# Forming half of the low weight parts with an accumulating DMA instead of VectorE

## The chip, the cores and the metric

The kernel runs on one core of one Trainium2 chip. The metric is the device time of one execution in microseconds (us). Engines are named as the profile names them: PE (TensorE, the matrix engine; PEld is its weight load), DVE (VectorE), ACT (ScalarE), POOL (GpSimd) and SP (SyncE). SPq, ACTq and POOLq are the sequencers that issue DMAs; all DMAs run on the core's 16 DMA engines.

## What is computed

Two decoder layers on 256 tokens of width 2048, in float32. Layer 0 mixes tokens by differential attention, layer 1 by a gated linear recurrence; each layer then has a squared-ReLU MLP (2048 to 8192 and back) and a gated embedding. Cut to what matters here:

```
for i in range(DEPTH):                       # DEPTH = 2
    xn = rmsnorm(h, g_mix[i])
    mix = diff_attention(xn, w_qkv, ...) if i % 2 == 0 else rglru_block(xn, w_in, ...)
    h = h + mix                              # both end in a product "@ w_o"
    h = h + square(relu(rmsnorm(h, g_mlp[i]) @ w_up[i])) @ w_down[i]
    ple_gate = sigmoid(rmsnorm(h, g_ple[i]) @ w_ple_gate[i])
    h = h + ple_gate * (p[i] @ w_ple_proj[i])
```

With 256 tokens, each weight is used once and read from memory once; nearly all the work is products with weights.

## The kernel before

**Precision.** A float32 operand is split into a high part (rounded to the short mantissa of float32r) and a low part, the rest. A product is then three matmuls, hi·hi, hi·lo and lo·hi. Line numbers are those of the profile of the kernel before.

**Tiling.** A `Group` (L60) is one product of 256 tokens with 512 columns. Its weights come in `Chunk`s of four k-tiles (512 rows of 512 columns, 1 MB), each loaded by one DMA on SP (L351) into a raw tile `w_raw`, of which there are three. A chunk is used as two `Sub`s of two k-tiles; the text calls them its even half (k0 = 0) and its odd half (k0 = 2). Each half is split into `w_hi` and `w_lo` tiles of 128x1024 elements, of which there are four each. `split` (L253) does that: ACT casts `w_raw` to `w_hi` (L255), and DVE subtracts, `w_lo = w_raw - w_hi` (L256).

**Order of the work.** `stream` (L332) walks over the halves of all groups. At half j it asks for loads two chunks ahead (L371), then for the split of half j + 3 (`split_to`, L374), then issues the matmuls of half j. With four buffers, the split of half j + 3 writes the tiles that the matmuls of half j - 1 have read, so it can start when these have ended, and must be done when the matmuls of half j + 3 begin: three halves later. In the products of the layout `flip` (L378, the MLP's up products) a half is 16 matmuls with the weights as the stationary operand; in the others (`mm3`, L248) it is 12 matmuls with the weights as the moving operand. Evictions, transposes, norms and softmax are deferred by some halves (`defer`, L115), so that they fall between the matmuls of later halves. Within the order in which the code is recorded, a scheduler may move instructions on DVE, ACT, PE and POOL; each engine then runs its own list in that order.

POOL does little: constants, the `rstd` powers of the norms (L265, L267, L310), and a few small loads (L150, L199, L413).

Some halves are not split this way: gate weights of layer 1 go through `own` (L887, a chunk without a source array), and the small `w_ple_proj` chunks have an even half only.

Of the kernel before, what the change touches and what calls it, by code (L numbers as in the profile page):

```python
# [11 lines left out]
AF = mybir.ActivationFunctionType  # L12
ALU = mybir.AluOpType
# [4 lines left out]
P = 128  # L18
# [9 lines left out]
EPS = 1e-6  # L28
KT_D = D // P
KC = 4  # L30
SK = 2
# [9 lines left out]


class Chunk:
    """Up to KC k-tiles of one weight column block, moved by one DMA."""

    def __init__(self, src, nk):
        self.nk, self.raw, self.pre = nk, None, None
        self.pieces = [(lambda raw: raw[:, :nk], src)]


class Sub:
    """SK k-tiles of a chunk, split into two float32r parts."""

    own = None

# [2 lines left out]


class Group:  # L60
    """One product over nk k-tiles: [256 tokens, 512 columns], or its transpose where flip is set."""

    def __init__(self, w, k0, nk, n0, lhs, evict, flip=False):
        self.lhs, self.evict, self.nk, self.flip, self.subs, self.pre = lhs, evict, nk, flip, [], {}
# [9 lines left out]
def trunk_kernel(ctx: ExitStack, tc, a, out):  # L74
    nc = tc.nc
# [4 lines left out]
    wk = ctx.enter_context(tc.tile_pool(name="wk", bufs=2))  # L80

    def t4(shape, dtype=F32):
        """4 KiB a partition"""
        return wk.tile(shape, dtype, tag="t4", name="t4", bufs=3)

    def v4(shape, dtype=F32):
# [6 lines left out]
        return wk.tile(shape, dtype, tag="t1", name="t1", bufs=3)  # L93

    def big(shape, dtype=F32):
        """8 KiB a partition"""
        return wk.tile(shape, dtype, tag="big", name="big", bufs=4)

    sm = ctx.enter_context(tc.tile_pool(name="sm", bufs=4))
# [7 lines left out]
    x = a["x"][0]  # L107
    p = a["p"]
    o_v = out[0].rearrange("(t p) d -> p t d", p=P)

# [1 line left out]
    state = {"tick": 0}  # L112
    pending = []

# [9 lines left out]
                pending.remove(e)  # L124
                e[2]()

# [1 line left out]
    h = cp.tile([P, NT, D], F32, name="h")  # L128
    x_v = x.rearrange("(t p) d -> p t d", p=P)

# [62 lines left out]
        nc.vector.tensor_scalar_mul(gss, g_sub, 1.0 - LAM0)  # L193

    def lam_setup():
        """lambda of the differential attention, the same on every partition"""
        lamv = t2([P, 4, DK])
        for i, nm in enumerate(("lam_q1", "lam_k1", "lam_q2", "lam_k2")):
            nc.gpsimd.dma_start(lamv[:, i], a[nm][0].partition_broadcast(P))  # L199

        def finish():
            lamm = t1([P, 2, DK])
            nc.vector.tensor_tensor(lamm, lamv[:, 0::2], lamv[:, 1::2], op=ALU.mult)
            lams = sm.tile([P, 2], F32, name="lams", bufs=1)
            nc.vector.tensor_reduce(lams, lamm, axis=AX.X, op=ALU.add)
            lame = sm.tile([P, 2], F32, name="lame", bufs=1)
            nc.scalar.activation(lame, lams, AF.Exp)
            nc.vector.tensor_tensor(neg_lam, lame[:, 1:2], lame[:, 0:1], op=ALU.subtract)
            nc.vector.tensor_scalar(neg_lam, neg_lam, LAM0, None, op0=ALU.subtract)

        defer(4, finish)

    def mask_setup():
        """-(query - key) where the key is visible, else a huge negative number"""
        nc.gpsimd.iota(
            mtab, pattern=[[-P, NT], [1, SEQ]], base=0, channel_multiplier=-1, allow_small_or_imprecise_dtypes=True
        )
        nc.gpsimd.affine_select(
            mtab, mtab, pattern=[[P, NT], [-1, SEQ]], compare_op=ALU.is_ge, fill=NEG, base=0, channel_multiplier=1
        )  # L220

    # 8 * softplus(-lam): log1p(u) = 2 atanh(u / (2 + u)) with u = exp(-|lam|)
    sp8 = cp.tile([P, 16], F32, name="sp8")
    nsp8 = cp.tile([P, 16], F32, name="nsp8")

# [18 lines left out]
        nc.vector.tensor_scalar_mul(sp8, ser, 8.0)  # L244
        nc.vector.tensor_scalar_mul(nsp8, ser, -8.0)

# [1 line left out]
    def mm3(ps, lh, ll, rh, rl, start, stop):  # L248
        nc.tensor.matmul(ps, lhsT=lh, rhs=rh, start=start, stop=False)  # L249
        nc.tensor.matmul(ps, lhsT=lh, rhs=rl, start=False, stop=False)  # L250
        nc.tensor.matmul(ps, lhsT=ll, rhs=rh, start=False, stop=stop)  # L251

    def split(hi, lo, src):  # L253
        """src = hi + lo exactly, each part of float32r's 12 significant bits."""
        nc.scalar.copy(hi, src)  # L255
        nc.vector.tensor_tensor(lo, src, hi.bitcast(F32), op=ALU.subtract)  # L256

# [2 lines left out]
        nc.vector.scalar_tensor_tensor(lo, in0=src, scalar=scale, in1=hi.bitcast(F32), op0=ALU.mult, op1=ALU.subtract)  # L260

    def rstd(ss, n, width, name):
        """(ss / width + EPS) ** -0.5 of [P, n]"""
        m = sm.tile([P, n], F32, name=name + "_m")
        nc.gpsimd.tensor_scalar(m, ss, 1.0 / width, EPS, op0=ALU.mult, op1=ALU.add)  # L265
        r = sm.tile([P, n], F32, name=name + "_r")
        nc.gpsimd.tensor_tensor(r, m, mhalf[:, :n], op=ALU.pow)  # L267
        return r

    def x32(shape):  # L270
        """32 KiB a partition"""
        return xp.tile(shape, F32R, tag="x32", name="x32")

    class Operand:
        """A split [k, token] operand of nk k-tiles."""

        def __init__(self, hi, lo):
            self.hi, self.lo = hi, lo
# [2 lines left out]
            return self.hi[:, kt, t * P : (t + 1) * P], self.lo[:, kt, t * P : (t + 1) * P]  # L281

    class Wide(Operand):
        """Both parts of a k-tile side by side: one [k, 512] moving operand."""

        def __init__(self):
            self.both = x32([P, KT_D, 2, SEQ])
            self.hi, self.lo = self.both[:, :, 0], self.both[:, :, 1]

    class Norm(Wide):  # L290
        """The rmsnorm of h as a transposed, split operand; the row factor r goes onto the products."""

        def __init__(self, gcol):
            super().__init__()
# [33 lines left out]
            for b in range(2):  # L328
                defer(1 + b, lambda b=b: self.transpose(nb, b))

# [1 line left out]
    def stream(groups):  # L332
        subs = [s for g in groups for s in g.subs]
        chunks = []
# [19 lines left out]
        def split_to(i):  # L354
            while done["split"] < min(i + 1, len(subs)):
                s = subs[done["split"]]
                load_to(cidx[id(s.chunk)])
                if s.own is not None:
                    s.own(s)
                else:  # L360
                    s.hi = wsp.tile([P, SK, NB], F32R, name="w_hi")
                    s.lo = wsp.tile([P, SK, NB], F32R, name="w_lo")
                    split(s.hi, s.lo, s.chunk.raw[:, s.k0 : s.k0 + SK])
                done["split"] += 1

        j = 0
        for g in groups:
            acc = [psum([P, NB]) for _ in range(4 if g.flip else NT)]
            kt = 0
            for i, s in enumerate(g.subs):  # L370
# [7 lines left out]
                if g.flip:  # L378
                    x = g.lhs()
                    for f in range(4):  # L380
                        fs = slice(f * P, (f + 1) * P)
                        for kk in range(SK):
                            k = kt + kk
# [10 lines left out]
                else:  # L394
                    for t in range(NT):
                        for kk in range(SK):
                            k = kt + kk
# [7 lines left out]

    groups = []

# [1 line left out]
    pT = {}  # L409

    def p_setup(l):
# [10 lines left out]

        defer(4, transpose)

# [1 line left out]
    n0 = Norm(G_MIX)  # L426

    attnT = [[big([P, 4, 3, P], F32R) for _ in range(2)] for _ in range(2)]
# [37 lines left out]
        return evict  # L466

    def softmax(ps, heads, t, nk):
        """attn = softmax(c = 0) - lam * softmax(c = 1) of [P, heads, 2, nk] scores"""
        n = len(heads)  # L470
        s = t2([P, n, 2, nk])
        for i, hd in enumerate(heads):
            nc.vector.scalar_tensor_tensor(
                s[:, i],
                in0=mtab[:, t, :nk].unsqueeze(1).broadcast_to([P, 2, nk]),
                scalar=2.0 ** -(hd + 1),
                in1=ps[:, i],
                op0=ALU.mult,
                op1=ALU.add,
            )  # L480
        s2 = s.rearrange("p n c k -> p (n c) k")
        nm = sm.tile([P, 2 * n], F32, name="nm")
        nc.vector.tensor_reduce(nm, s2, axis=AX.X, op=ALU.max)
        nc.vector.tensor_scalar_mul(nm, nm, -1.0)
        z = sm.tile([P, n, 2], F32, name="z")
        zf = z.rearrange("p n c -> p (n c)")
        for i in range(2 * n):
            nc.scalar.activation(s2[:, i], s2[:, i], AF.Exp, bias=nm[:, i : i + 1], accum_out=zf[:, i : i + 1])
        nc.vector.reciprocal(zf, zf)
        nc.vector.tensor_scalar_mul(z[:, :, 1], z[:, :, 1], neg_lam)  # L490
        at = t1([P, n, nk])
        for i in range(n):
            nc.vector.tensor_scalar_mul(s[:, i, 1], s[:, i, 1], z[:, i, 1:2])
            nc.vector.scalar_tensor_tensor(
                at[:, i], in0=s[:, i, 0], scalar=z[:, i, 0:1], in1=s[:, i, 1], op0=ALU.mult, op1=ALU.add
            )
        return at
# [93 lines left out]
                )  # L591

    def residual_evict(nb, norm, scale=None):
        """h += product; the last contribution to this block feeds the next norm."""

        def evict(acc):
            add_to_h(acc, nb, scale)
            if norm is not None:
                norm().feed(nb)

        return evict
# [20 lines left out]
    for nb in range(4):  # L622
        groups.append(Group(a["w_o_attn"][0], 0, KT_D, nb * NB, lambda kt, t: oT().lhs(kt, t), residual_evict(nb, n_mlp0)))

# [1 line left out]
    FC = 1024  # L626
    NFC = DFF // FC
    FKT = FC // P
# [1 line left out]
    def mlp(l, norm_in, norm_out):  # L630
        hid = {}

        def up_evict(c, half):
            """relu(.) ** 2 of a transposed product; the row factor squared goes onto the next product"""

            def evict(acc):
                if half == 0:
# [32 lines left out]
            down(c - 1)  # L670
        down(NFC - 1)

# [1 line left out]
    def ple(l, norm_in, norm_out):  # L674
        pps, sgs = {}, {}

# [45 lines left out]
    n_mix1 = later(lambda: Norm(G_MIX + 16))  # L722
    ple(0, n_ple0, n_mix1)

# [1 line left out]
    w_in = a["w_in_rec"][0]  # L726
    rg = {}
    yT = later(Wide)
# [5 lines left out]
        return rg  # L734

    def gate_weights():
        """They lie in the k-tiles of yT that come last."""
        w = yT().both[:, 8:16]
        return w[:, :, 0], w[:, :, 1]

# [61 lines left out]
        return evict  # L802

    def recur(half):
        """a = exp(-s r), b = sqrt(1 - a^2) i x with 1 - a^2 = tanh(s r) (1 + a^2); then the scan"""

        def decay(q):
            for c in range(4 * q, 4 * q + 4):
# [62 lines left out]
        return evict  # L871

    def gate_chunk(nb):
        """The gate weights of 512 channels: they go through the weight stream's loads and splits."""
        ch = Chunk(None, KC)
        v = lambda raw: raw.rearrange("p k n -> p (k n)").rearrange("p (n g k j) -> p n g k j", n=2, g=2, k=2)
        ch.pieces = [
# [1 line left out]
                lambda raw, n=n, g=g: v(raw)[:, n, g],  # L879
# [28 lines left out]
    mlp(1, n_mlp1, n_ple1)  # L908
    ple(1, n_ple1, None)

    # the first group takes x as it comes
    first = groups[0]
    chunks = [first.subs[i].chunk for i in range(0, len(first.subs), KC // SK)]
    w0 = w_qkv[: KC * P, :NB].rearrange("(c p) n -> p c n", p=P)
# [62 lines left out]
```

## Time and profile before

| | |
|---|---|
| median of 3 timed runs | 2328.12 us (2327.57 to 2328.15) |
| span of the profiled execution (its own time, first to last instruction) | 2326.8 us |
| PE busy | 2308.8 us, 99% |
| DVE busy | 1424.6 us, 61% |
| ACT busy | 1193.6 us, 51% |
| POOL busy | 44.7 us, 2% |
| weight loads on SP (queue q1), share of 16 DMA engines | 57.3% |
| read from HBM | 435 MB |

The table gives shares of the whole span. An engine at 99% sets the time; the others cost only where PE waits for them. The profile shows this with its idle times: PE's groups have almost none before them.

### The profile page before, as it was taken

The numbers are of one execution on the slowest core, as the hardware profiler recorded it, in microseconds if no ns is written. First come the engines' busy times: TensorE is split into PE (matmuls) and PEld (weight loads), VectorE is DVE, ScalarE is ACT, GpSimd is POOL, SyncE is SP. The second block draws the span as 40 slices with busy tenths as digits, with TensorE's granted clock in tenths as the row PEclk, the third lists the DMA queues.
The fourth block names the chain that finished last, engine by engine and source line by source line (L and its number), as shares of the span: only waits on it lengthen the run. The fifth ranks groups of instructions, "written<-read, shape, count | busy, mean of one in ns | idle before, by whom it ended". The sixth has DMA issues, their size and how long they took to land.

```text
span 2326.8 us, 28564 instructions
## 1 busy us (share of the span) xinstructions
PE 2308.8 (99%) x11467; PEld 1946.9 (84%) x11467; DVE 1424.6 (61%) x1704; ACT 1193.6 (51%) x1594; POOL 44.7 (2%) x79
## 2 busy tenths in 40 slices
PE   8999999999999999999999999999999999999999
PEld 6888888888888888888888887888888888888887
DVE  6676655565565665566566767566565555565654
ACT  6555554444444444444558887454444444444453
POOL 2100000000000000000000000000000000000000
PEclk9999999999999999999999999999999999999999
DMA  7454555555565655655566565556565565555554
GB/s 241 163 185 163 165 179 181 185 195 189 191 197 184 198 188 192 196 185 181 189 193 219 187 212 181 181 182 198 184 197 190 191 197 184 198 189 191 177 199 148
DMA packets 225396, 438.95 MB, mean 189 GB/s; under 512 B 7582, under 2 KB 16416, under 8 KB 225264
## 3 DMA queue, kind: packets, MB, share of 16 engines
q1 hardware_dynamic: 224608, 436.24, 57.3%
q8 instruction: 89, 1.46, 0.3%
q0 software_dynamic: 608, 0.89, 0.2%
q14 instruction: 43, 0.35, 0.0%
q10 hardware_dynamic: 48, 0.02, 0.0%
HBM read 435.01 MB, written 2.10 MB: 188 GB/s over the span
## 4 chain that ended last, share of the span: by engine, by line
PE 94%; DVE 2%; ACT 2%; DMA 1%; issue 1%; SPq 0%; POOL 0%; DVEq 0%; ACTq 0%
PE acc L391 31%; PE acc L251 21%; PE acc L249 20%; PE acc L250 20%; PE tp L317 1%; DVE w_lo L256 1%; ACT w_hi L255 1%; DMA w_raw<-in_w_gate_x_dram 0%; DVE t L770 0%; DMA h<-in_x_dram 0%; PE tp L458 0%; DVE big L827 0%; ACT L810 0%; SPq L351 0%; ACT L788 0%
## 5 line engine op out<-in xcount | busy, mean ns | idle before, releaser
L256 DVE TENSOR_TENSOR w_lo<-w_raw,w_hi 128x1024 fp32r<-128x1024 f32 x808 | 987.4, 1224 | 781.4 <-ACT w_hi L255 779.9
L255 ACT CAST w_hi<-w_raw 128x1024 fp32r<-128x1024 f32 x808 | 849.0, 1052 | 979.8 <-PE acc L251 605.7
L391 PE MATMUL acc<-x,w_hi 128*128 128x512 f32 x2048 | 704.8, 394 | 0.0
L391 PE MATMUL acc<-x,w_lo 128*128 128x256 f32 x2048 | 547.8, 278 | 0.0
L249 PE MATMUL acc<-w_hi,x 128*128 128x512 f32 x1152 | 457.1, 397 | 0.0
L250 PE MATMUL acc<-w_lo,x 128*128 128x512 f32 x1152 | 450.2, 391 | 1.9 <-DVE w_lo L256 1.8
L251 PE MATMUL acc<-w_hi,x 128*128 128x512 f32 x1152 | 450.5, 391 | 0.0
L391 PEld LDWEIGHTS acc<-x,w_hi 128*128 128x128 f32 x2048 | 376.0, 188 | 78.6
L249 PE MATMUL acc<-w_hi,big 128*128 128x512 f32 x1024 | 399.7, 390 | 0.0
L251 PE MATMUL acc<-w_hi,big 128*128 128x512 f32 x1024 | 398.6, 389 | 0.0
L250 PE MATMUL acc<-w_lo,big 128*128 128x512 f32 x1024 | 398.4, 389 | 0.0
L391 PEld LDWEIGHTS acc<-x,w_lo 128*128 128x128 f32 x2048 | 384.7, 188 | 11.2
L251 PEld LDWEIGHTS acc<-w_hi,x 128*128 128x128 f32 x1152 | 216.8, 188 | 46.8 <-DVE x L256 0.2
L250 PEld LDWEIGHTS acc<-w_lo,x 128*128 128x128 f32 x1152 | 217.2, 189 | 45.0 <-DVE w_lo L256 3.0
L249 PEld LDWEIGHTS acc<-w_hi,x 128*128 128x128 f32 x1152 | 216.8, 188 | 41.7
L251 PEld LDWEIGHTS acc<-w_hi,big 128*128 128x128 f32 x1024 | 192.2, 188 | 40.3
L250 PEld LDWEIGHTS acc<-w_lo,big 128*128 128x128 f32 x1024 | 192.3, 188 | 39.8
L249 PEld LDWEIGHTS acc<-w_hi,big 128*128 128x128 f32 x1024 | 192.2, 188 | 39.0
L589 DVE SCALAR_TENSOR_TENSOR h<-acc,n_r,h 128x512 f32<-128x512 f32 x128 | 89.9, 744 | 0.0
L644 ACT COPY t<-acc 128x256 f32<-128x256 f32 x128 | 47.5, 371 | 22.8 <-PE acc L391 20.6
L259 ACT ACTIVATE x<-tp,cols_a 128x256 fp32r<-128x256 f32 (+1 forms) x72 | 35.7, 496 | 39.5 <-DVE x L260 39.5
L260 DVE SCALAR_TENSOR_TENSOR x<-tp,cols_a,x 128x256 fp32r<-128x256 f32 (+1 forms) x72 | 36.8, 511 | 18.8 <-ACT x L259 18.8
(173 smaller groups left out, 1064.2 us busy)
## 6 DMA issues: line engine op xcount, KB each, us to landing
w_raw<-in_w_up_dram SPq DMA_DIRECT2D x128, 1024.0 KB, 5.2
w_raw<-in_w_down_dram SPq DMA_DIRECT2D x128, 1024.0 KB, 5.1
w_raw<-in_w_qkv_dram SPq DMA_DIRECT2D x47, 1024.0 KB, 5.2
w_raw<-in_w_ple_gate_dram SPq DMA_DIRECT2D x32, 1024.0 KB, 5.2
w_raw<-in_w_in_rec_dram SPq DMA_DIRECT2D x32, 1024.0 KB, 5.5
w_raw<-in_w_o_attn_dram SPq DMA_DIRECT2D x16, 1024.0 KB, 5.2
w_raw<-in_w_o_rec_dram SPq DMA_DIRECT2D x16, 1024.0 KB, 5.1
w_raw<-in_w_ple_proj_dram SPq DMA_DIRECT2D x8, 512.0 KB, 3.7
```

The costliest lines, as they stand in the source:

```text
L249: nc.tensor.matmul(ps, lhsT=lh, rhs=rh, start=start, stop=False)
L250: nc.tensor.matmul(ps, lhsT=lh, rhs=rl, start=False, stop=False)
L251: nc.tensor.matmul(ps, lhsT=ll, rhs=rh, start=False, stop=stop)
L255: nc.scalar.copy(hi, src)
L256: nc.vector.tensor_tensor(lo, src, hi.bitcast(F32), op=ALU.subtract)
L259: nc.scalar.activation(hi, src, AF.Copy, scale=scale)
L260: nc.vector.scalar_tensor_tensor(lo, in0=src, scalar=scale, in1=hi.bitcast(F32), op0=ALU.mult, op1=ALU.subtract)
L317: nc.tensor.transpose(tp[:, i, t * P : (t + 1) * P], h[:, t, (k0 + i) * P : (k0 + i + 1) * P], ident)
L391: nc.tensor.matmul(o, lhsT=lh, rhs=rh, start=k == 0 and n == 0, stop=k == g.nk - 1 and n == 1)
L589: nc.vector.scalar_tensor_tensor(hb, in0=acc[t], scalar=scale()[:, t : t + 1], in1=hb, op0=ALU.mult, op1=ALU.add)
L644: nc.scalar.copy(other, ps[:, SEQ:])
```

## The change

The weight source is kept in the chunk. For the even half nothing changes. For the odd half of every chunk that has a source array, three operations stand where two stood: ACT writes the negated rounded weights into `w_lo` (L367 of the changed kernel), ACT casts the same raw weights into `w_hi` (L368), and POOL issues a DMA (L369) that reads the same 128x2x512 weights from HBM once more and adds them to `w_lo`, so that `w_lo = -hi + w`. The subtraction on DVE is gone for these halves. The rest of the diff drops docstrings and comments; lines behind L369 are six higher than before.

```
     def __init__(self, src, nk):
-        self.nk, self.raw, self.pre = nk, None, None
+        self.nk, self.raw, self.pre, self.src = nk, None, None, src
...
                     s.hi = wsp.tile([P, SK, NB], F32R, name="w_hi")
                     s.lo = wsp.tile([P, SK, NB], F32R, name="w_lo")
-                    split(s.hi, s.lo, s.chunk.raw[:, s.k0 : s.k0 + SK])
+                    raw = s.chunk.raw[:, s.k0 : s.k0 + SK]
+                    if s.k0 == 0 or s.chunk.src is None:
+                        split(s.hi, s.lo, raw)
+                    else:
+                        nc.scalar.activation(s.lo, raw, AF.Copy, scale=-1.0)
+                        nc.scalar.copy(s.hi, raw)
+                        nc.gpsimd.dma_start(s.lo, s.chunk.src[:, s.k0 : s.k0 + SK], accum_op=ALU.add)
                 done["split"] += 1
```

How the instructions move is shown at three places. The first is ACT in the MLP of layer 0, around the eviction of an up product (`t1<-acc` are its copies, `big` the split of its result); a raw tile's number tells which two halves belong to one chunk. Before:

```order
L255 CAST w_hi_5305<-w_raw_5283 128x1024
L255 CAST w_hi_5327<-w_raw_5283 128x1024
L255 CAST w_hi_5347<-w_raw_5325 128x1024
L644 COPY t1_5370<-acc_5195 128x256
L644 COPY t1_5373<-acc_5196 128x256
L644 COPY t1_5380<-acc_5197 128x256
L644 COPY t1_5383<-acc_5198 128x256
L255 CAST w_hi_5395<-w_raw_5325 128x1024
L255 CAST big_5367<-t2_5369 128x512
L255 CAST w_hi_5415<-w_raw_5393 128x1024
```

And the same place in the changed kernel:

```order
L255 CAST w_hi_5413<-w_raw_5390 128x1024
L367 ACTIVATE w_lo_5436<-w_raw_5390 128x1024
L368 CAST w_hi_5435<-w_raw_5390 128x1024
L255 CAST w_hi_5456<-w_raw_5433 128x1024
L650 COPY t1_5479<-acc_5300 128x256
L650 COPY t1_5482<-acc_5301 128x256
L650 COPY t1_5489<-acc_5302 128x256
L367 ACTIVATE w_lo_5505<-w_raw_5433 128x1024
L650 COPY t1_5492<-acc_5303 128x256
L368 CAST w_hi_5504<-w_raw_5433 128x1024
L255 CAST big_5476<-t2_5478 128x512
L255 CAST big_5476<-t2_5488 128x512
```

ACT has three operations of 128x1024 for a chunk in place of two; the negated copy stands ahead of the cast of the same half.

The second place is ACT at the start of the program, where the first chunks are split (the difference of the two lists; `h` is the residual stream, `n_ss` the sums of squares of the first norm):

```order
 L302 ACTIVATE t_150,n_ss<-h 128x512
-L255 CAST w_hi<-w_raw 128x1024 x3
+L367 ACTIVATE w_lo<-w_raw 128x1024
+L368 CAST w_hi<-w_raw 128x1024
+L255 CAST w_hi<-w_raw 128x1024
+L368 CAST w_hi<-w_raw 128x1024
+L367 ACTIVATE w_lo<-w_raw 128x1024
 L259 ACTIVATE x_101<-tp,cols_g 128x256
```

The first odd half's negated copy stands where its cast stood; in the second chunk the cast comes first.

The third place is POOL in the attention's projections (`q_m`, `q_r` and `o_m` are the powers of the norms; all `w_lo` rows are accumulating DMAs):

```order
+L369 DMA w_lo<-in_w_qkv_dram 128x2x512 x4
 L265 TENSOR_SCALAR q_m<-q_ss 128x8
 L267 TENSOR_TENSOR q_r<-q_m,mhalf 128x8
+L369 DMA w_lo<-in_w_qkv_dram 128x2x512 x4
 L265 TENSOR_SCALAR q_m<-q_ss 128x8
 L267 TENSOR_TENSOR q_r<-q_m,mhalf 128x8
+L369 DMA w_lo<-in_w_qkv_dram 128x2x512 x4
```

POOL's list has 400 rows more, all accumulating DMAs; they stand in the same list as the norms' powers. The list of SP's loads keeps its order.

## Rows read from the trace of the kernel before

**Rows 1.** The page: busy time, share of the span and instructions of each engine.

```profile
PE 2308.8 (99%) x11467; PEld 1946.9 (84%) x11467; DVE 1424.6 (61%) x1704; ACT 1193.6 (51%) x1594; POOL 44.7 (2%) x79
```

**Rows 2.** The page's groups: line, engine, op, out<-in, xcount | busy us, mean ns | idle before.

```profile
L256 DVE TENSOR_TENSOR w_lo<-w_raw,w_hi 128x1024 fp32r<-128x1024 f32 x808 | 987.4, 1224 | 781.4 <-ACT w_hi L255 779.9
L255 ACT CAST w_hi<-w_raw 128x1024 fp32r<-128x1024 f32 x808 | 849.0, 1052 | 979.8 <-PE acc L251 605.7
...
L250 PE MATMUL acc<-w_lo,x 128*128 128x512 f32 x1152 | 450.2, 391 | 1.9 <-DVE w_lo L256 1.8
```

**Rows 3.** The chain that ended last: start us, length us, what (longest pieces).

```profile
537.50 44.40 PE acc L391 x256
625.42 44.40 PE acc L391 x256
...
2088.84 44.40 PE acc L391 x256
```

**Rows 4.** Timeline of ACT and DVE within an MLP: start us, length us, engine, line, operation.

```profile
1004.90 1.05 ACT L255 CAST w_hi<-w_raw 128x1024 fp32r<-128x1024 f32 x1 [1.10 <-PE acc L391]
1005.98 1.23 DVE L256 TENSOR_TENSOR w_lo<-w_raw,w_hi 128x1024 fp32r<-128x1024 f32 x1 [0.94 <-ACT w_hi L255]
1007.67 1.05 ACT L255 CAST w_hi<-w_raw 128x1024 fp32r<-128x1024 f32 x1 [1.72 <-PE acc L391]
```

**Rows 5.** DMA queues and issues in the MLP's window 460 to 1047 us.

```profile
q1 hardware_dynamic: 56337, 111.88, 58.4%
...
w_raw<-in_w_down_dram SPq DMA_DIRECT2D x57, 1024.0 KB, 5.2
w_raw<-in_w_up_dram SPq DMA_DIRECT2D x50, 1024.0 KB, 5.2
```

**Rows 6.** Stretches: window, length, busy PE, PEld, DVE, ACT, POOL, PEclk, DMA share, GB/s.

```profile
5.00:10.00 5.00, 1.42 (x6) 0.72 (x4) 2.68 (x4) 2.36 (x4) 3.06 (x6) 1.00 1.02 343
10.00:15.00 5.00, 3.69 (x11) 3.13 (x12) 0.88 (x2) 2.56 (x7) 0.09 (x1) 1.00 1.05 390
460.00:1047.00 587.00, 587.00 (x2998) 499.87 (x2998) 346.63 (x378) 259.31 (x298) 0.00 (x0) 1.00 0.59 191
1215.00:1460.00 245.00, 240.88 (x1187) 201.15 (x1186) 174.47 (x230) 197.88 (x282) 1.93 (x7) 1.00 0.61 198
```

**Rows 7.** DMA issues of the whole span: KB each, median us from issue to landing.

```profile
w_raw<-in_w_ple_proj_dram SPq DMA_DIRECT2D x8, 512.0 KB, 3.7
...
h<-in_x_dram SPq DMA_DIRECT2D x3, 512.0 KB, 11.2
...
t<-in_p_dram POOLq DMA_DIRECT2D x2, 256.0 KB, 3.4
```

**Rows 8.** POOL's issue of the load of p: duration ns min/median/max.

```profile
L413 POOL DMA_DIRECT2D t<-in_p_dram x2: 778/789/800, 133.9 to 1191.9; - x2
```

**Rows 9.** Timeline of the start: splits and first matmuls.

```profile
14.39 2.94 ACT L255 CAST w_hi<-w_raw 128x1024 fp32r<-128x1024 f32 x3
...
15.46 3.50 DVE L256 TENSOR_TENSOR w_lo<-w_raw,w_hi 128x1024 fp32r<-128x1024 f32 x3 [1.64 <-ACT w_hi L255]
...
17.44 0.71 PE L249 MATMUL acc<-w_hi,x 128*128 128x512 f32 x2
```

**Rows 10.** Groups of ACT and DVE in layer 1's mixer, 1215 to 1460 us.

```profile
L255 ACT CAST w_hi<-w_raw 128x1024 fp32r<-128x1024 f32 x77 | 79.9, 1048 | 25.8 <-PE acc L251 25.4
...
L822 ACT ACTIVATE big<-big 128x1024 f32<-128x1024 f32 x4 | 4.2, 1058 | 0.0
...
L256 DVE TENSOR_TENSOR w_lo<-w_raw,w_hi 128x1024 fp32r<-128x1024 f32 x76 | 92.1, 1221 | 32.7 <-ACT w_hi L255 32.7
```

**Rows 11.** Groups of ACT in the window 460 to 1047 us.

```profile
L255 ACT CAST w_hi<-w_raw 128x1024 fp32r<-128x1024 f32 x214 | 225.5, 1054 | 318.4 <-PE acc L251 164.6 <-PE acc L391 153.8
```

## The prediction

> **What bounds the kernel now.** I read the busy times first: PE is busy 2308.8 us of a span of 2326.8, DVE 61%, ACT 51%, POOL 2% [rows 1]. Only 18 us are left in which PE does nothing, so no relief of another engine can give back more than that. The page's groups say the same from the other side: the matmuls that read w_lo waited 1.8 us in all for DVE's subtraction, while DVE itself idled 781 us waiting for ACT's cast, and ACT idled 980 us, mostly until PE set a buffer free [rows 2]. So the split runs ahead of PE and is held back by it. The chain of waits gives the pace in the MLPs: 256 matmuls of an up product pair (16 halves) take 44.40 us, 2.775 us a half, and the next such piece starts 87.92 us after the last, 32 halves later: 2.75 us a half on average, 5.495 us a chunk [rows 3]. The MLPs have 256 of the 400 chunks that the change touches. The timeline shows the reserve of the split there. The cast starts when PE ends half j - 1, the subtraction ends 2.31 us later (1004.90 to 1007.21) [rows 4], and the result is wanted when half j + 3 starts, 3 x 2.75 = 8.25 us after the cast's start: 5.9 us to spare.
>
> The DMA engines come next, since the change puts its load there. In the window 460 to 1047 us the weight loads fill 58.4% of all 16 engines with 107 chunks, so one chunk takes 0.584 x 587 / 107 = 3.20 us of the 16 engines [rows 5]. At the start, when the engines are full (shares 1.02 and 1.05), they move 343 and 390 GB/s, by which a chunk of 1.049 MB takes 3.06 or 2.69 us [rows 6].
>
> **What goes.** 400 subtractions on DVE of 1.224 us [rows 2], 490 us of busy time, beside a PE that does not wait for them: worth nothing in the MLPs, and at most the 18 us of PE's idle time anywhere.
>
> **What comes on ACT.** 400 negated copies. The operation with a scale is not in the trace on this shape; the cast of the same shape takes 1.054 us [rows 11] and an activation of that shape in layer 1's mixer 1.058 [rows 10], so I take 1.06. In an MLP that is 107 x 1.06 = 113 us on top of 259 in 587 us [rows 6]: 63%, covered by ACT's 318 us of waiting for PE there [rows 11]. In layer 1's mixer (1215 to 1460 us) it is not covered so well: 77 casts mean some 38 odd halves, 40 us on top of 198 in 245 [rows 6, 10], so ACT is at 97% while PE already has 4 us of idle time there. Bounds: minus 4 (DVE loses 38 x 1.22 = 46 us there, and PE's idle time goes) to plus 40 (none of the new copies finds a gap). I take 2, since ACT's wait for PE before the casts alone is 25.8 us there and there are further waits to fill.
>
> **What comes on POOL.** 400 issues. POOL's own issue of a 256-row transfer takes 0.79 us [rows 8]; one per 5.5 us fills 14% of an almost empty engine. Each issue waits for its negated copy, and the norms' powers queue behind it. They wait for at most one such copy and issue, some 2 us, and the factors are wanted at an eviction several halves away: nothing.
>
> **What comes on the DMA engines.** 400 transfers of 512 KB, 210 MB on top of 435. The accumulating form does not stand in the trace, so its cost is bounded. From below: it costs what a plain transfer of 512 KB does, half a chunk, 1.35 to 1.60 us of the 16 engines. Together with the chunk's load 4.04 to 4.80 us, below the pace of 5.495: hidden. The middle value: an addition needs the old w_lo as well as the weights, two operands of 512 KB for one result, so it costs the engines what 1 MB costs, 2.69 to 3.20 us; with the load 5.38 to 6.40 us against 5.495, which is at the edge or over it. From above: nothing in the rows excludes a slower path still; the slowest 512 KB transfer, the load of x into full queues, took 11.2 us to land [rows 7]. I take the middle value, because it follows from what the operation must read, and the rows for it are the 1 MB loads.
>
> The Trainium skill, page "Collectives: The Full Stack", section "The bandwidth ceiling: the fold count and why AG ≠ RS ≠ AR", says of additions in the DMA path that the add itself costs no cycles, but that its two source reads go through one ring, so that it delivers half the rate of a copy. No run here shows an accumulation so far; the plain row of 512 KB above would let the change end near 2333 us, the rule at the sum below.
>
> **The wait that decides.** The chain of an odd half is now: PE ends half j - 1, negated copy 1.06, DMA from issue to landing L, then PE's own half 2.75, and four halves of PE must hold this: 4 x 2.75 = 11.0. So the change is hidden as long as L is at most 11.0 - 1.06 - 2.75 = 7.2 us; beyond it the chunk takes (3.81 + L) / 2. A plain 512 KB transfer lands in 3.7 us [rows 7], a 1 MB one in 5.2 [rows 5]. The accumulation does not run alone: the load into the raw tile that this same half sets free is issued within about a microsecond of it, and shares all 16 engines. A plain cost gives L = 3.7 + 1.35 to 1.60 = 5.1 to 5.3, hidden with 1.9 to spare. The double cost gives L = 5.2 + 2.69 to 3.20 = 7.9 to 8.4, so the chunk takes 5.85 to 6.1 us, 0.36 to 0.61 more than now. Over 256 chunks that is 91 to 156 us; I take the middle, 124. The other 144 chunks have (2326.8 - 256 x 5.495) / 144 = 6.4 us each, or 6.2 without the start and the few small chunks, because PE does transposes, scores and gates between their halves: 5.85 to 6.1 us fits, and I count nothing.
>
> **The start.** The first chunks are split while PE waits for them. The second half's w_lo is ready at about 16.6 us (15.46 and one subtraction) and its matmuls begin about 17.4 [rows 9]. In the changed order the negated copy stands in the cast's place, ends at 15.4, and the DMA lands 5.2 to 8.4 us later among full queues, at 20.6 to 23.8: PE begins 3.2 to 6.4 us later, and since it never waits again, the loss stays. I take 5.
>
> **The sum.** 2326.8 + 124 + 5 + 2 = 2457.8. The profiled execution's span stands 1.3 us below the median of the runs shown; with that the forecast is 2459 us, PE waiting for accumulating DMAs.
>
> **The rivals.**
> Hidden: the accumulation costs about what a copy costs, L stays near 5, and PE keeps its pace in the MLPs. For it: PE's reserve of 5.9 us and 41.6% free DMA time. Against it: the start and the mixer still cost something, 0 to 10 us in all. That gives 2328 to 2340 us; I split it into no change (2328) and a small loss, which reaches 2400 if some transfers land late.
> Slower path: accumulation takes several times a copy. With L = 11.2 a chunk takes 7.5 us: 256 x 2.0 + 144 x 1.3 = 700 us more, 3030. For it: nothing in the trace shows the form, and its result is rounded to another type on the way. Against: L must be over three times that of a plain 512 KB.
> Faster: in layer 1's mixer DVE's share falls, PE's 4.1 us of idle time there go, and with them some 3 of the other 14 at the start and the end. It decides only if the accumulation is cheap enough to stay hidden everywhere (L below 7.2) and the start loses nothing; then 2328.1 - 7 = 2321 us. Against it: ACT, not DVE, is the fuller engine there, and it is ACT that gets the copies.
> That the change does not do what it says I rule out: 400 transfers more stand in POOL's list and 400 subtractions fewer in DVE's.
>
> **How the numbers follow.** Forecast (DMA path at double cost, 2400 to 2600; its ends are the cheapest wait above, and a queue held at 6.40 us a chunk, 256 x 0.9 + 144 x 0.2 = 260 more): 0.47. Hidden, a small loss of 2333 to 2400: 0.22. Hidden, no change: 0.15. Slower path, beyond 2600: 0.13. Faster: 0.03. What can be told from no change is 0.2%, 4.7 us. So faster 0.03, same 0.15, slower 0.47 + 0.22 + 0.13 = 0.82. The range that holds 8 in 10 takes the forecast, the small losses, half of no change and the lower half of the slower path: 2328 to 2720.
>
> **What would show it.** The profile after should show 400 w_lo DMAs on a POOL queue with about 210 MB; DVE's L256 down to 408 and ACT up by about 420 us; DMA share above 90% in the MLPs; PE idle before the matmuls that read w_lo, released by DMA w_lo, in odd halves alone; a chunk of 5.85 to 6.1 us where it was 5.5; and landings of 7.9 to 8.4 us. Landings near 5 us with PE still at 99% would make the forecast wrong by the step on double cost; landings well above 9 us would make it wrong by the same step on the other side. PE waits that name ACT in the mixer beyond a few us would upset that term.

## The result and the profile after

The changed kernel takes 2821.03 us (median of 4 runs, 2813.96 to 2831.86) against 2327.85 us: 1.2122 times as long (95% interval 1.2096 to 1.2148), 493 us more. The forecast was 2459 us and slower; the sign was right, the size was not, and the range (to 2720) did not hold it. The profiled execution has a span of 2812.1 us at a mean granted clock of 0.975.

The page before has this chain by engine (the shares of the work that ended last):

```profile
PE 94%; DVE 2%; ACT 2%; DMA 1%; issue 1%; SPq 0%; POOL 0%; DVEq 0%; ACTq 0%
```

The page after: busy times (they answer to [rows 1]), the two DMA queues (q1 has SP's loads, q0 POOL's transfers), the chain by engine, DVE's subtractions, and two groups of matmuls that read w_lo ([rows 2] has one of them before).

```profile
PE 2441.1 (87%) x11467; PEld 1986.9 (71%) x11467; DVE 967.8 (34%) x1304; ACT 1553.7 (55%) x1992; POOL 519.7 (18%) x479
...
q1 hardware_dynamic: 224608, 436.24, 49.5%
q0 software_dynamic: 109408, 210.63, 42.5%
...
DMA 55%; PE 27%; issue 10%; ACT 7%; DVE 1%; POOL 1%; SPq 0%; POOLq 0%; ACTq 0%; DVEq 0%
...
L256 DVE TENSOR_TENSOR w_lo<-w_raw,w_hi 128x1024 fp32r<-128x1024 f32 x408 | 499.5, 1225 | 1442.0 <-ACT w_hi L255 1441.5
...
L397 PE MATMUL acc<-x,w_lo 128*128 128x256 f32 x2048 | 571.4, 289 | 115.7 <-DMA w_lo<-in_w_up_dram 115.2
...
L250 PE MATMUL acc<-w_lo,big 128*128 128x512 f32 x1024 | 414.2, 405 | 120.4 <-DMA w_lo<-in_w_down_dram 120.0
```

The 400 subtractions are gone as counted (987.4 to 499.5 us in DVE's group). The busy time of DVE as a whole fell by 457 us and that of ACT rose by 360, less than the 490 and 420 that were counted. But the chain that was 94% PE is now 55% DMA, and the matmuls that read w_lo, which had waited 1.8 us for DVE, now wait more than 230 us for the accumulating DMAs in these two groups alone. By q0's share an accumulation takes 0.425 x 2812.1 / 400 = 2.99 us of the 16 engines; by q1's share and its 436 MB a chunk's load of 1.049 MB takes about 3.35.

The loads of w_down in layer 0 give the pace: issues by line, with first and last start. First the kernel before:

```profile
L351 SPq DMA_DIRECT2D w_raw<-in_w_down_dram x64: 367/368/368, 474.4 to 1084.3; - x64
```

Then the changed kernel:

```profile
L351 SPq DMA_DIRECT2D w_raw<-in_w_down_dram x64: 367/368/368, 538.7 to 1294.4; - x64
```

The same stretch of work takes 755.7 us in place of 609.9; at 5.495 us a chunk before [rows 3] that is 6.81 us a chunk.

The four pairs of `w_hi` and `w_lo` buffers are used in turn, each again after four halves; the text calls this the ring. A transfer has landed when its semaphore says that the data are there. One turn of the ring can be read in the timeline of the changed kernel. The rows are the negated copy of an odd half, the issue of its DMA, the first matmul that reads its w_lo, and the next negated copy into the same buffer.

```profile
1005.24 1.06 ACT L367 ACTIVATE w_lo<-w_raw 128x1024 fp32r<-128x1024 f32 x1 [1.77 <-PE acc L250]
...
1006.60 1.19 POOL L369 DMA_DIRECT2D w_lo<-in_w_down_dram  x1 [4.83 <-ACT w_lo L367]
...
1015.95 0.50 PE L250 MATMUL acc<-w_lo,big 128*128 128x512 f32 x1 [1.67 <-DMA w_lo<-in_w_down_dram]
...
1018.57 1.06 ACT L367 ACTIVATE w_lo<-w_raw 128x1024 fp32r<-128x1024 f32 x1 [3.44 <-PE acc L250]
```

Copy 1.06, handing over 0.30, DMA from 1006.60 to about 1015.8, the half on PE, and the buffer is free 13.3 us after the copy began. Four halves of PE take 11.0. The prediction's ring is there, with a longer DMA in it: two chunks in 13.3 us are 6.7 us a chunk.

### The profile page after: what moved, and what is told of

Same layout as the page of the kernel before. It is cut to its first block, busy times and chain, and to the rows that moved or that the text cites. A ratio compares the mean times of both kernels' runs of the same rounds, so it can differ in the third digit from the quotient of the medians.

```text
span 2812.1 us, 29666 instructions
## 1 busy us (share of the span) xinstructions
PE 2441.1 (87%) x11467; PEld 1986.9 (71%) x11467; DVE 967.8 (34%) x1304; ACT 1553.7 (55%) x1992; POOL 519.7 (18%) x479
## 4 chain that ended last, share of the span: by engine, by line
DMA 55%; PE 27%; issue 10%; ACT 7%; DVE 1%; POOL 1%; SPq 0%; POOLq 0%; ACTq 0%; DVEq 0%
DMA w_lo<-in_w_down_dram 20%; DMA w_lo<-in_w_up_dram 19%; PE acc L250 7%; PE acc L397 7%; PE acc L251 6%; PE acc L249 6%; ACT w_lo L367 5%; DMA w_lo<-in_w_qkv_dram 4%; DMA w_lo<-in_w_ple_gate_dram 4%; DMA w_lo<-in_w_in_rec_dram 3%; DMA w_lo<-in_w_o_attn_dram 2%; DMA w_lo<-in_w_o_rec_dram 2%; DMA w_raw<-in_w_gate_x_dram 1%; ACT w_hi L255 0%; DVE w_lo L256 0%
## 5 line engine op out<-in xcount | busy, mean ns | idle before, releaser
L256 DVE TENSOR_TENSOR w_lo<-w_raw,w_hi 128x1024 fp32r<-128x1024 f32 x408 | 499.5, 1225 | 1442.0 <-ACT w_hi L255 1441.5
L367 ACT ACTIVATE w_lo<-w_raw 128x1024 fp32r<-128x1024 f32 x400 | 424.2, 1060 | 783.1 <-PE acc L250 511.6
L397 PE MATMUL acc<-x,w_hi 128*128 128x512 f32 x2048 | 732.6, 403 | 0.0
L397 PE MATMUL acc<-x,w_lo 128*128 128x256 f32 x2048 | 571.4, 289 | 115.7 <-DMA w_lo<-in_w_up_dram 115.2
L250 PE MATMUL acc<-w_lo,x 128*128 128x512 f32 x1152 | 470.4, 408 | 113.5 <-DMA w_lo<-in_w_in_rec_dram 31.2
L250 PE MATMUL acc<-w_lo,big 128*128 128x512 f32 x1024 | 414.2, 405 | 120.4 <-DMA w_lo<-in_w_down_dram 120.0
L249 PE MATMUL acc<-w_hi,x 128*128 128x512 f32 x1152 | 464.7, 405 | 0.0
L251 PE MATMUL acc<-w_hi,x 128*128 128x512 f32 x1152 | 462.1, 401 | 0.0
L368 ACT CAST w_hi<-w_raw 128x1024 fp32r<-128x1024 f32 x400 | 414.4, 1036 | 15.6 <-PE acc L251 15.6
L369 POOL DMA_DIRECT2D w_lo<-in_w_down_dram x128 | 152.7, 1193 | 722.5 <-ACT w_lo L367 608.4
L369 POOL DMA_DIRECT2D w_lo<-in_w_up_dram x128 | 152.6, 1192 | 711.9 <-ACT w_lo L367 562.6
L251 PEld LDWEIGHTS acc<-w_hi,x 128*128 128x128 f32 x1152 | 224.2, 195 | 46.3
L249 PEld LDWEIGHTS acc<-w_hi,x 128*128 128x128 f32 x1152 | 223.2, 194 | 45.1
```

What stands on the lines that cost most here:

```text
L367: nc.scalar.activation(s.lo, raw, AF.Copy, scale=-1.0)
L368: nc.scalar.copy(s.hi, raw)
L369: nc.gpsimd.dma_start(s.lo, s.chunk.src[:, s.k0 : s.k0 + SK], accum_op=ALU.add)
L397: nc.tensor.matmul(o, lhsT=lh, rhs=rh, start=k == 0 and n == 0, stop=k == g.nk - 1 and n == 1)
```

## The experiments

**Adding against copying.** The first two runs vary what the DMA does.

```
-  nc.gpsimd.dma_start(s.lo, s.chunk.src[:, s.k0 : s.k0 + SK], accum_op=ALU.add)
+  nc.gpsimd.dma_start(s.lo, s.chunk.src[:, s.k0 : s.k0 + SK])                    # copy_not_add
+  nc.gpsimd.dma_start(s.lo, raw, accum_op=ALU.add)                               # add_from_raw
```

> The DMA of the odd half copies the weights into w_lo instead of adding them to it (so w_lo is not the low part; what is left out is the addition alone). Issue, waits, bytes read from HBM and bytes written stay. Theory A, the addition is what is dear, because it needs two operands: a transfer takes the engines half of the 2.99 us that it takes now, about 1.5, landing falls from 9.0 to about 6 us, a chunk goes back to 5.5 us in the MLPs, and the time to 2330 to 2360 us. Rival B, the queue of POOL (its issue of 1.19 us, its way of making descriptors) is what is dear: landing stays at 8 to 9 us and the time at 2700 to 2820 us.

Measured: 2418.14 us, 1.0389 times before (1.0359 to 1.0419), 403 us less than with the addition. So the accumulating form is most of the price. Its page has the queues and the landings:

```profile
q1 hardware_dynamic: 224608, 436.24, 49.4%
q0 software_dynamic: 109408, 210.63, 36.0%
...
w_lo<-in_w_up_dram POOLq DMA_DIRECT2D x128, 512.0 KB, 4.5
w_lo<-in_w_down_dram POOLq DMA_DIRECT2D x128, 512.0 KB, 6.5
```

The same bytes take 0.360 x 2417.3 / 400 = 2.18 us of the engines, not the 1.5 that was expected, and the time missed the expected 2330 to 2360. Rival B (2700 to 2820) is refuted; whether the queue has a share in the 90 us that are left, no run separates.

> The accumulating DMA takes its weights from the raw tile in SBUF, not from HBM a second time. Theory A, the price is the two operands that each engine must read, wherever they lie: engine time per transfer stays near 3 us and the time at 2700 to 2830 us. Rival C, the second reading of HBM is the price (645 MB in place of 435): engine time falls towards 2 us, landing to about 7, and the time to 2340 to 2500 us. The raw tile is held until the DMA has landed, so if loads become late as well the time can rise above 2830.

Measured: 2600.72 us, 1.1173 times before (1.1078 to 1.1269), between both expectations. The engine time of a transfer stays (43.3% of 2608.3 us, 2.82 us each), as theory A has it: reading SBUF in place of HBM does not make the addition cheap for the engines. But it lands in 6.1 us in the median, not 9.0, and now ACT waits for late loads as well (119.0 and 100.2 us before w_hi, for the loads of w_down and w_up), since the raw tile must be held until the DMA has read it. Engine time and time to land are two things.

**Why it lands late.** The DMA view of short windows of the changed kernel, after the issue at 1006.60 above. First 1008.0 to 1010.4 us, then 1011.5 to 1014.3: queue, packets, MB, share of the 16 engines.

```profile
q1 hardware_dynamic: 389, 0.76, 101.3%
q0 software_dynamic: 2, 0.00, 0.0%
...
q0 software_dynamic: 175, 0.36, 69.6%
q1 hardware_dynamic: 171, 0.35, 38.1%
```

And the copy run, issue at 1005.72 us, window 1007.0 to 1009.5:

```profile
q0 software_dynamic: 257, 0.50, 85.5%
q1 hardware_dynamic: 50, 0.10, 11.2%
```

Up to 1010.4, 3.8 us after the issue, the accumulation has moved no data while the load of the next raw tile has all engines. Then the two queues take turns, packet by packet (175 and 171 in 2.8 us), an added packet of 2 KB at 0.696 x 2.8 x 16 / 175 = 178 ns and a loaded one at 100 ns: 16 pairs on each engine are 4.4 us. The copy had moved all its packets 3.8 us after its issue. By the packet records of the 400 transfers of each trace, the first data packet stands 3.9 us behind the issue for an accumulation and 1.4 for a copy, and the last one ends at 8.5 and 4.6 (medians). A load on SP has its first packet 1.0 us behind its issue in the kernel before.

The 3.9 us are not a property of the accumulation alone: what goes ahead is the load of the next raw tile. The run `every_second`, which is explained below, has two cases side by side. First the issues on POOL and of the next load on SP in the one case, then in the other:

```profile
827.14 1.20 POOL L369 DMA_DIRECT2D w_lo<-in_w_up_dram  x1 [12.61 <-ACT w_lo L367]
827.80 0.37 SPq L351 DMA_DIRECT2D w_raw<-in_w_up_dram  x1
...
840.28 1.19 POOL L369 DMA_DIRECT2D w_lo<-in_w_up_dram  x1 [11.94 <-ACT t L650]
841.21 0.37 SPq L351 DMA_DIRECT2D w_raw<-in_w_down_dram  x1
```

The DMA view from 1.8 to 3.2 us after POOL's issue, 829.0 to 830.4 us and then 842.1 to 843.5:

```profile
q1 hardware_dynamic: 117, 0.24, 75.4%
...
q0 software_dynamic: 58, 0.12, 67.5%
q1 hardware_dynamic: 14, 0.03, 19.7%
```

With the load issued 0.66 us behind it, the accumulation moves nothing in these 1.4 us (its first packet comes at 3.95 us); with the load 0.93 us behind it, it starts at 1.9. In the 196 transfers of that trace, 112 had a load issued at most 0.7 us behind them: none began before 3.0 us, and they landed after 9.15 us (median). 76 had it 0.87 to 2.5 us behind: 74 began before 2.0, at 1.9 in the median, and the 76 landed after 7.2 us, which is about what the prediction's ring allows. The changed kernel shows the same: 0 of 282 and 53 of 101 began before 2.0 us. So an accumulation is ready 1.9 us after its issue, a copy 1.4, and a load issued 0.66 us behind it, whose first packet comes 1.0 us later at about 1.7, falls between the two. In the copy run 263 of 272 copies with a load 0.5 to 0.7 us behind them began at 1.4. The difference of 0.5 us is as large as that of POOL's two issues, accumulation first, copy second:

```profile
L369 POOL DMA_DIRECT2D w_lo<-in_w_down_dram x128 | 152.7, 1193 | 722.5 <-ACT w_lo L367 608.4
...
L369 POOL DMA_DIRECT2D w_lo<-in_w_down_dram x128 | 91.7, 716 | 631.1 <-ACT w_lo L367 539.4
```

No run shows that the longer issue is the reason, and none tries what the kernel would take if SP issued its load a little later. The next run takes bytes away and leaves the issue as it is.

```
-  nc.gpsimd.dma_start(s.lo, s.chunk.src[:, s.k0 : s.k0 + SK], accum_op=ALU.add)
+  nc.gpsimd.dma_start(s.lo[:, :, :128], s.chunk.src[:, s.k0 : s.k0 + SK, :128], accum_op=ALU.add)
```

> The accumulating DMA moves 128 of the 512 columns only (128 KB; the other columns of w_lo keep the negated high part, which leaves out three quarters of the additions). ACT's copies, POOL's issues and all waits stay. If transfer size is what costs (A, R and D alike): engine time under 1.2 us, landing 4 to 5 us, and 2330 to 2350 us, with 3 to 15 us left for the start and layer 1's mixer. If ACT's 400 copies or POOL's issues have a share of the loss, it shows here as a time above 2360.

Measured: 2439.58 us, 1.0481 times before (1.0451 to 1.0512), outside the 2330 to 2350 that all theories expected. The landing:

```profile
w_lo<-in_w_up_dram POOLq DMA_DIRECT2D x128, 128.0 KB, 6.8
w_lo<-in_w_down_dram POOLq DMA_DIRECT2D x128, 128.0 KB, 6.9
```

A quarter of the bytes lands in 6.8 us, not 4 to 5: the first packet still stands 3.6 us behind the issue in the median. So size is not all of it. The other branch of the expectation, that ACT's copies or POOL's issues have a share, is priced further down for ACT: 13 us. The last pair of runs below splits each transfer by rows.

**Ring or full engines.** The DMA engines are busy 94% of the time in the changed kernel's MLP (460 to 1320 us), so either could set the pace.

```profile
q1 hardware_dynamic: 66897, 132.86, 50.4%
q0 software_dynamic: 34544, 66.59, 43.4%
```

The next run gives each transfer more time without changing its work.

```
+  # odd halves: all matmuls that read s.hi first, those that read s.lo last
+  for part in (1, 0):          # flip: part 1 reads s.hi, part 0 reads s.lo
+      ...
```

> In odd halves PE does the matmuls that read w_hi first and those that read w_lo last, so that w_lo may be 1.8 us later; bytes, transfers and waits stay. Theory R, the ring of buffers sets the pace (four halves hold the negated copy 1.06, handing over 0.3, landing 9.1 and what PE does after it, 2.75 of a half now, 0.92 then): four halves take 11.4 in place of 13.2 us, a chunk 5.7, and the time falls to 2400 to 2500 us. Rival D, the DMA engines are simply full (3.35 us for the load and 2.99 for the addition, 6.34 of some 6.8 us a chunk): the transfers land later by as much, a chunk stays at 6.4 or more, and the time is 2600 to 2800 us.

Measured: 2667.37 us, 1.146 times before (1.1339 to 1.158). 154 us are gone, not the 320 or more of theory R; the time lies in rival D's range. The DMA view of its MLP (427 to 1220 us) says why it stops there:

```profile
q1 hardware_dynamic: 65384, 129.85, 52.9%
q0 software_dynamic: 33654, 64.90, 46.6%
```

Together 99.5%. With the ring loosened the engines are full: that is a floor, and the changed kernel lies above it, or these 154 us could not have gone. The test that parts the two is half the transfers.

```
-  if s.k0 == 0 or s.chunk.src is None:
+  if s.k0 == 0 or s.chunk.src is None or cidx[id(s.chunk)] % 2 == 0:
```

> Only every second chunk's odd half is accumulated (200 transfers in place of 400); the other chunks are split as before. Theory D, the DMA engines' work sets the pace: an average chunk needs 3.3 + 1.5 = 4.8 us of them, under the 5.5 us of PE, so the loss nearly vanishes: 2330 to 2400 us. Rival R, the ring of buffers: one late transfer in four halves costs what two cost (each is 9.0 + 0.3 us after a copy of 1.06 where 7.2 are free, some 2 us late), so the loss stays at 250 to 450 us.

Measured: 2722.01 us, 1.1693 times before (1.1669 to 1.1716): half the transfers (196 of them by the trace, where the text before the run says 200) keep 394 of the 493 us. Its loads of w_down in layer 0, and the DMA view of its MLP (427 to 1250 us):

```profile
L351 SPq DMA_DIRECT2D w_raw<-in_w_down_dram x64: 367/368/368, 516.8 to 1267.6; - x64
...
q1 hardware_dynamic: 64111, 127.31, 48.0%
q0 software_dynamic: 16348, 31.49, 22.0%
...
w_lo<-in_w_up_dram POOLq DMA_DIRECT2D x32, 512.0 KB, 9.1
w_lo<-in_w_down_dram POOLq DMA_DIRECT2D x29, 512.0 KB, 9.0
```

The stretch takes 750.8 us, 6.76 us a chunk against 6.81 with all transfers. The engines have 30% free, and the transfers still land after 9 us. Full engines can't explain this; the ring can, since one late transfer in four halves stretches the turn as much as two.

> The same 200 transfers, and in the accumulated halves PE does the matmuls that read w_lo last, which gives each transfer 1.8 us more. If the ring is what is left at half the transfers, its 2 us of lateness fall to 0.2: 2335 to 2400 us. If this stays near the run without the later matmuls, lateness is not the cause there.

Measured: 2425.21 us, 1.0418 times before (1.0397 to 1.0439). The same 196 transfers cost 97 us instead of 394 when PE wants them 1.8 us later. That is lateness, shown at equal transfers and equal bytes. The time is 25 us above the expected 2400; what these 25 us are was not separated.

**ACT's part and the start.**

```
-  nc.gpsimd.dma_start(s.lo, s.chunk.src[:, s.k0 : s.k0 + SK], accum_op=ALU.add)
+  nc.vector.tensor_tensor(s.lo, raw, s.hi.bitcast(F32), op=ALU.subtract)         # act_part_only
...
-  if s.k0 == 0 or s.chunk.src is None:
+  if s.k0 == 0 or s.chunk.src is None or cidx[id(s.chunk)] < 8:                  # start_plain
```

> In the odd halves ACT writes the negated copy as in the changed kernel, but then DVE forms w_lo by its subtraction as before; no accumulating DMA. This prices ACT's 400 copies alone. The prediction's term was 2 us (bounds minus 4 to 40). The copy run lost 28 us in layer 1's mixer and 38 in the MLPs. Theory A1, the mixer's loss is ACT's: 2345 to 2360 us, all of it in the mixer. Rival, it is the transfers' (their landing, not ACT): within 5 us of before.

Measured: 2341.43 us, 1.0058 times before (1.0041 to 1.0075): ACT's 400 copies, and the cast that stands behind each of them, cost 13 us by themselves (10 to 17). The mixer shows most of it, 1215 to 1475 us, with PE's group of transposes that waits there:

```profile
1215.00:1475.00 260.00, 247.90 (x1195) 204.52 (x1194) 176.49 (x231) 225.44 (x315) 2.07 (x7) 0.99 0.58 188
...
L767 PE MATMUL tp<-ident,t 128*128 128x128 f32 x32 | 5.4, 282 | 7.5 <-ACT t L754 5.9 <-DVE t L871 1.1 <-ACT t L772 0.5
```

PE has 12 us of idle time there, where it had 4 before [rows 6]; 5.9 us of it are waits for ACT's L754.

> The first eight chunks are split as before, the other 392 are accumulated. This prices the start: the prediction's term was 5 us. In the changed kernel's trace PE waits 7.8 us for the first accumulated w_lo. Expected: 8 to 15 us less than the changed kernel's 2821 us, 2800 to 2815; that the start costs nothing of its own would leave it at 2821.

Measured: 2795.02 us (2789.75 to 2800.30), 26 us less than the changed kernel: more was saved than the expected 2800 to 2815 allow. But the runs of both kernels spread by 10 us and more, which leaves 14 to 42. The stretch 0 to 60 us shows the mechanism; first the changed kernel, with the matmul that waits:

```profile
0.00:60.00 60.00, 44.48 (x196) 35.82 (x197) 23.06 (x59) 35.71 (x60) 20.90 (x35) 0.94 0.94 256
...
23.85 0.79 PE L250 MATMUL acc<-w_lo,x 128*128 128x512 f32 x1 [7.77 <-DMA w_lo<-in_w_qkv_dram]
```

And the run with a plain start:

```profile
0.00:60.00 60.00, 51.96 (x235) 42.03 (x236) 37.63 (x76) 37.94 (x64) 14.07 (x29) 1.00 0.77 242
```

The first accumulated w_lo is used at 23.85 us, and more waits follow; 39 fewer matmuls are done by 60 us. By the issues of SP's loads the changed kernel is 14 us behind this run at its 15th load (83.6 against 69.4 us) and still 14 us at the end (2784.2 against 2770.6 for the last load). So the start costs about 14 us, as expected; the rest of the 26 is not explained by these traces, whose own spans are 13.6 us apart.

**What the delay is made of.** Each transfer as two DMAs of 128 rows:

```
-  nc.gpsimd.dma_start(s.lo, s.chunk.src[:, s.k0 : s.k0 + SK], accum_op=ALU.add)
+  for kk in range(SK):
+      k1 = s.k0 + kk
+      nc.gpsimd.dma_start(s.lo[:, kk : kk + 1], s.chunk.src[:, k1 : k1 + 1], accum_op=ALU.add)
```

> Each accumulated half is fetched by two DMAs of one k-tile (128 rows, 256 KB) instead of one of 256 rows. In the changed kernel the first packet of a transfer stands 4.0 us behind its issue, where a copy's stands 1.5 us behind. If that delay is made of the rows (descriptors written before any may start), the first DMA's packets start near 2.5 us, the second's are prepared meanwhile, the last lands at 7.5 to 8.3 us in place of 9.0, and the time falls to 2650 to 2760 us, where the engines' 6.3 to 6.4 us a chunk stop it. If it is a fixed cost of an accumulating DMA, two of them land later, at 9.5 us or more, and the time rises to 2830 to 3000 us.

Measured: 2699.90 us, 1.1595 times before (1.1561 to 1.1629), the time that the first case expected.

```profile
w_lo<-in_w_up_dram POOLq DMA_DIRECT2D x256, 256.0 KB, 7.0
w_lo<-in_w_down_dram POOLq DMA_DIRECT2D x256, 256.0 KB, 7.2
```

These medians mix two kinds. In the packet records the first DMA of each pair has its first packet 1.7 us behind its issue, and 269 of the 400 begin before 2.0 us; in the MLPs it lands after 4.7 to 4.9 us. The second begins 5.0 us behind its own issue. Together they land 8.4 to 8.8 us behind the first issue, where the undivided transfer took 9.0 to 9.2. So the time came out as expected, but the last landing did not (7.5 to 8.3), and the delay before the first packet is not one fixed length for a DMA or for its rows: it hangs on what is ahead in the engines.

> Half the transfers, with the matmuls that read w_lo last, and each transfer as two DMAs: the least harmful form of this change so far. With landing below 8 us the ring is loose: 2345 to 2400 us, what is left being the start (some 25 us in the full change) and ACT's share. Not expected to be faster than the kernel before, since PE has nothing to gain. If the delay before the first packet is fixed for each DMA, 2425 to 2500 us.

Measured: 2417.67 us, 1.0383 times before (1.033 to 1.0435), no clear difference from the run with one DMA each, and above the 2400 of the first case, below the 2425 of the second. The least harmful form still costs 89 us; nothing here beats the kernel before, whose PE has 18 us of idle time in all to give back.

## Why the prediction was wrong

- **What bounds the kernel, and what goes.** Nothing speaks against it: no run took the subtractions away without putting something in their place, and none came out faster than the kernel before.
- **Engine cost of an addition.** Right in its middle value: 2.69 to 3.20 us were forecast, 2.99 measured; the copy run shows 2.18 for the same bytes. In packets this trace has 178 ns against 100 ns of a load, a factor of 1.8. The page "Collectives: The Full Stack" of the Trainium skill, in its section "The bandwidth ceiling: the fold count and why AG ≠ RS ≠ AR", puts the ReduceScatter of a ring at half the rate of the AllGather, since the add needs two source reads; the factor here is near it.
- **The wait that decides: the step that failed.** The ring, (3.81 + L) / 2 a chunk, was the right equation, and L was mis-sized. I built L from a 1 MB load's landing on SP (5.2 us) plus the load beside it (2.69 to 3.20): 7.9 to 8.4. It is 9.0 to 9.2, with 0.3 for handing over that I had left out. The sum hid what is in L. The load that I took as its model has its first packet 1.0 us behind its issue; an accumulation is ready 0.9 us later than that, at 1.9, and is then late for the engines: the next load is ahead, and the first packet comes at 3.9 us in the median. From there to the last data packet it takes 4.7, in turns with the load. Past 7.2 us each microsecond of L costs 0.5 us in every chunk. With 9.1 + 0.3 the equation gives 6.6 us; measured are 6.81. The rest, 0.2 us a chunk, is not separated; PE's clock is one candidate: at a mean granted clock of 0.975 some 2 x 0.025 x 2812 = 141 us ran at the lower level (an estimate from that mean), and a half on PE is part of each turn. In the MLPs this term was forecast at 124 us and is 256 x (6.81 - 5.495) = 337, by layer 0's pace.
- **The other 144 chunks** were counted at nothing, since 5.85 to 6.1 us fit into their 6.2. At 6.6 and more they don't fit: they carry what is left of the loss, 493 - 337 - 14 - 13 = 129 us (a difference). The issues of SP's loads in the traces of before and after agree with it: 35 us are lost in the attention behind the start, 87 between the two MLPs (ACT's part included) and 19 behind the second.
- **The start** was forecast at 5 us and cost about 14. The first late w_lo was priced well: it is used at 23.85 us, 5.9 behind the 17.99 of the kernel before. I left out the ones that follow.
- **ACT in the mixer:** 2 us forecast, 13 measured, within the bounds of minus 4 to 40. ACT's wait for PE, which I took as room, did not cover all of the copies.
- **POOL** was counted at nothing, with 0.79 us an issue; the accumulating issue took 1.19. Whether these 0.4 us put it behind the load was argued above and not shown by a run. DVE's waits for the norms' powers rose from 21.7 to 35.4 us in all; whether any of it reached PE was not separated.
- **The rivals.** "Hidden" is refuted by the landing of 9 us, and in the copy run even a plain copy costs 90 us. The "slower path" had 0.13 and named the right place, L, with too slow a transfer. Full engines, the upper end of my forecast's own case (260 us), turned out to be a floor under the changed kernel: it shows when the ring is loosened (99.5% busy, 2667 us) and is not what sets 2821: half the transfers leave 30% of the engines free and keep the pace in the MLP.

What stays open: of the 89 us that the least harmful form costs, the issues of the loads place some 40 in the MLPs, 34 between them (13 or less are ACT's) and 19 ahead of them, in a profiled execution that is 94 us longer than before; what each of these is, and likewise the 90 us of the copy run, was not separated.

## What to carry to other kernels

Before moving work from an engine that waits to DMA, write down the ring of buffers with the time to land in it, and put the delay before the first packet into that time as a term of its own; a transfer of another kind on another queue is no model for it. Then ask which transfer the same event sets off beside it and which of the two has its first packet earlier: here 0.2 us decided whether a whole load went ahead. Halving the number of transfers tells a late transfer from full engines: if the loss stays, it is lateness, and using the result later is worth more than moving fewer bytes: here 297 us against 99. By the same equation another buffer would give time too; no run tried that.

## What the runs showed of the hardware

An accumulating DMA from POOL occupies POOL for 1.19 us for 256 rows, a copy of the same shape for 0.72. Its first packet comes 1.9 us after the issue at the earliest, against 1.4; where the packets of a load stand ahead, it comes at some 4 us (3.97 in the median of the 282 cases above). Once both have begun, the two queues share the engines packet by packet (175 against 171 in the window above), so that a load beside an addition slows down as well: a 1 MB load lands in 8.3 to 8.6 us in the changed kernel's MLPs, where it took 5.2 [rows 5].

TensorE's clock is not steady through these waits. The changed kernel in windows of 2 us (PE busy is the second number, the granted clock the third from the end):

```profile
1026.00:1028.00 2.00, 1.53 (x7) 0.94 (x5) 0.00 (x0) 1.05 (x2) 0.95 (x1) 1.00 1.10 210
1028.00:1030.00 2.00, 0.00 (x0) 0.00 (x0) 1.22 (x1) 0.39 (x1) 0.00 (x0) 1.00 0.93 227
1030.00:1032.00 2.00, 1.53 (x4) 1.26 (x5) 0.00 (x0) 0.00 (x0) 0.00 (x0) 0.60 1.06 252
1032.00:1034.00 2.00, 2.00 (x7) 1.59 (x6) 0.00 (x0) 0.00 (x0) 0.00 (x0) 0.55 1.03 247
1034.00:1036.00 2.00, 2.00 (x10) 1.63 (x9) 0.00 (x0) 1.41 (x2) 0.05 (x1) 1.00 0.30 95
```

After a stall in which PE did nothing for 2.9 us (up to 1030.47), the next two windows ran mostly at the lower of the two levels, 1.2 GHz in place of 2.4, and PE got through 7 matmuls in 2 us where it does 10 at full clock. The shorter stall before 1015.95 (1.67 us) left it at 1.00, and so did one of 3.1 us before 2038.5: not every long stall costs clock.
